# A last matrix product in fp32 by seven half-size products in place of eight

## The chip, the cores and the metric

One core of a Trainium2 chip runs the whole program as one launch. The metric is the device time of that launch in microseconds (us). Shorter is better. The kernel before was timed three times, with a median of 1404.88 us (1404.58 to 1405.83).

## What is computed

The program is a two-layer encoder for 1024 tokens of 1024 features, in float32. Layer A (an mLSTM beside a pooling mixer) comes first, then layer C, an attention layer with 8 heads of 128 features. The change concerns only the end of layer C, its output projection and the residual:

```
def mla_layer(x, ...):                       # x: (1, 1024, 1024)
    ...
    o = block_causal_attention(q, k, v).reshape(B, S, C_WIDTH) * jax.nn.silu(z)
    return x + o @ w_out                     # w_out: (1024, 1024)
```

So the last step is out = x1 + O W, with O (tokens by features) of 1024 by 1024 and W of 1024 by 1024. x1 is the output of layer A.

## The kernel before

**Products.** TensorE multiplies float32 numbers that are rounded to a shorter format. To keep float32 precision the kernel writes each operand as a sum hi + lo of two rounded numbers (`split`, L153 to L161: hi is a rounding copy on POOL or on ACT, lo = src - hi is a subtraction on DVE), and computes three matmuls hi·hi, hi·lo and lo·hi per block (`mm3`, L172 to L178), all into one PSUM bank. One matmul takes 128 features by 128 tokens against 128 features by 512 columns.

**Layer C.** The eight heads of attention run one after the other. While head h computes, `ahead(h)` feeds in pieces of what head h+1 needs, and during the last head (h = 7) the generator `out_ahead` (L1228) loads and splits the first operands of the output projection. Every head's gated output z is stored to a scratch array oz_d in HBM (L1198, SP's DMA queue); this is O transposed, features by tokens. It comes back from there as the left operand. Per head, a row of key norms goes over POOL (`rk`, L213), SP's queue out to HBM (`rk_d`, L1071) and back as `rkb` (L1072), and the head's scores are scaled by it (L1158).

**Output projection before** (L1276 to L1312). Eight feature tiles k, eight token tiles j and two column halves ch make 8 x 16 blocks of three matmuls, 384 in all. Operands are rows of 128 features by 1024: eight of O (`os` split into `oh`, `ol`) and eight of W (`w_st` split into `w_hi`, `w_lo`; the first three, `woh` and `wol`, by `out_ahead`). All loads there go out on ACT's queue. The first 192 matmuls run k by k over eight PSUM banks (so that operands can arrive while PE works), the other 192 bank by bank. Each bank is evicted by one DVE addition with a row of x1 (`x1r`, L1311) and stored by SP (L1312).

**Order.** The source's order isn't the engines' order. A scheduler, which runs at build time, reorders the instructions of each engine (`TC_KW = dict(schedule_with_timeline_sim=True)`). On the chip each engine runs its queue strictly in that order and waits on semaphores where an operand is not ready or a buffer is not free.

Of the kernel before, what the change touches and what calls it, by code (L numbers as in the profile page):

```python
# [19 lines left out]
P = 128  # L20
# [28 lines left out]
OUT_AHEAD = 3  # L49
# [7 lines left out]
def _parts(value, bits, n):  # L57
    """value as a sum of n numbers of at most `bits` significant bits each."""
# [30 lines left out]
def _hybrid(ctx, tc, nc, ins, consts, out, dbg):  # L89
# [20 lines left out]
    # ---------------------------------------------------------------- constants  # L110
# [52 lines left out]
    def split_scaled(hi, lo, src, scale):  # L163
        """src * scale = hi + lo; src in PSUM, scale a number or a column."""
# [7 lines left out]
    def mm3(acc, terms, start=True, stop=True):  # L172
        """acc (+)= sum of lhs.T @ rhs over terms ((lhs_hi, lhs_lo), (rhs_hi, rhs_lo))."""
# [8 lines left out]
    def wload(shape, src, hi_eng="pool", own=None, into=None):  # L182
        """A block of weights, or of other operands, loaded and split."""
# [25 lines left out]
    def rstd_of(dst, ssq, n):  # L209
        """dst = (ssq / n + eps) ** -0.5 for small tiles."""  # L210
# [7 lines left out]
    # ================================================================ layer A  # L218
# [29 lines left out]
    def om_tile(h, sig, ws, j):  # L248
        """sigmoid(om) of a head for 128 tokens; with the last head's columns the gates too."""
# [12 lines left out]
    # ---- x normalised, transposed and split, and the first head's output gate on its heels  # L262
# [57 lines left out]
    def feat_pieces(c0, use, w=None):  # L320
        """128 columns of the projection, features on partitions: use(half, psum) per half."""
# [27 lines left out]
    def conv(h, c, xm):  # L349
        """SiLU of the causal convolution of a chunk."""  # L350
# [23 lines left out]
    def windows(g, x0s, half):  # L374
        """Trailing means less the value itself, split, for half of the tokens."""
# [44 lines left out]
    def gate_math():  # L420
# [4 lines left out]
        # Scratch in the room of tiles that come later.  # L425
# [13 lines left out]
        # log_sigmoid(f) = min(f, 0) - log1p(exp(-|f|))  # L439
# [10 lines left out]
        # Sums of log f within a tile of 128 tokens, and over whole tiles.  # L450
# [19 lines left out]
        # The running maximum within a tile, one (tile, head) per partition; then over tiles.  # L470
# [876 lines left out]
```

## Time and profile before

| what | value |
|---|---|
| median of three runs | 1404.88 us |
| span of the profiled execution (first to last instruction) | 1403.8 us, 1.1 us under that median |
| PE busy | 1374.9 us, 98% of the span |
| DVE / ACT / POOL busy | 755.2 / 475.0 / 412.0 us |
| granted TensorE clock, mean | 0.997 |
| first matmul of the output projection (f_ps) starts | 1309.39 us |
| last eviction of it (x1r) starts | 1400.20 us |

The output projection is `f_ps` in the trace, its evictions are `x1r<-f_ps,x1r` on DVE. The engines are PE (matmul), PEld (weight load), DVE, ACT, POOL and SP. In a timeline a row gives start, duration, engine, line, operation, output and inputs, and in brackets how long the engine sat idle before and what released it. A row "x3" stands for three instructions in a row, and its duration is the stretch that they take together. Of the profiled execution the page gives the span alone; what lies around it is set at the 1.1 us above.

### The profile page before, as it was taken

To read this page: it belongs to the slowest core of one execution; us is meant where nothing else is said; L and a number is where in the kernel's file an instruction comes from. 1 tells how busy PE (TensorE), PEld (TensorE's weight loads), DVE (VectorE), ACT (ScalarE), POOL (GpSimd) and SP (SyncE) were. 2 spreads that over 40 slices of the span, in tenths; PEclk is the share of its full clock that TensorE was granted. 3 is DMA by queue.
4 is the path that set the end of the run, shared out by engine and by line. 5 is a ranking of instruction groups with operands and counts; after the bars stand their busy time and mean duration, and the time that the engine had idled before them with its cause. 6 is when DMAs were issued, how large, how long until landed. Compare 5 with 4: busy or idle time off the path is not lost.

```text
span 1403.8 us, 20224 instructions
## 1 busy us (share of the span) xinstructions
PE 1374.9 (98%) x7740; PEld 1205.8 (86%) x7740; DVE 755.2 (54%) x1616; ACT 475.0 (34%) x1146; POOL 412.0 (29%) x546
## 2 busy tenths in 40 slices
PE   7999999999999999999999999999989999999998
PEld 6888789888998889888888889988889999988887
DVE  6686544663365544653655333640167777878631
ACT  5433223331432223320001112421376667675200
POOL 3155213441144212321533111420153324151310
PEclk9999999999999999999999999999999999999999
DMA  5122311133022311127834232231311211122541
GB/s 198 39 81 64 101 53 48 55 94 97 16 80 60 102 53 53 51 74 253 301 106 150 90 88 78 73 103 53 104 34 54 67 54 54 57 80 69 217 157 53
DMA packets 101406, 126.88 MB, mean 90 GB/s; under 512 B 6231, under 2 KB 72510, under 8 KB 101310
## 3 DMA queue, kind: packets, MB, share of 16 engines
q1 hardware_dynamic: 98574, 115.63, 25.9%
q10 hardware_dynamic: 2736, 9.96, 2.0%
q8 instruction: 61, 1.00, 0.3%
q14 instruction: 35, 0.29, 0.1%
HBM read 100.34 MB, written 25.24 MB: 89 GB/s over the span
## 4 chain that ended last, share of the span: by engine, by line
PE 88%; DVE 4%; POOL 2%; issue 2%; DMA 2%; ACT 2%; SPq 0%; DVEq 0%; ACTq 0%; POOLq 0%
PE fp_ps L178 8%; PE fp_ps L177 8%; PE fp_ps L176 8%; PE s_ps L1155 5%; PE o_ps L176 4%; PE o_ps L178 4%; PE o_ps L177 4%; PE z_ps L178 2%; PE z_ps L177 2%; PE z_ps L176 2%; PE f_ps L178 2%; PE f_ps L176 2%; PE f_ps L177 2%; PE om_ps L177 2%; PE om_ps L178 2%; PE om_ps L176 2%
## 5 line engine op out<-in xcount | busy, mean ns | idle before, releaser
L156 POOL TENSOR_SCALAR w_hi<-w_st 128x1024 fp32r<-128x1024 f32 (+4 forms) x131 | 134.2, 1025 | 555.8 <-PE fp_ps L177 136.7
L161 DVE TENSOR_TENSOR w_lo<-w_st,w_hi 128x1024 fp32r<-128x1024 f32 (+4 forms) x131 | 156.2, 1194 | 221.7 <-POOL w_hi L156 221.7
L178 PE MATMUL fp_ps<-xnh,w_lo 128*128 128x512 f32 x512 | 202.6, 398 | 0.8 <-DVE w_lo L161 0.7
L177 PE MATMUL fp_ps<-xnl,w_hi 128*128 128x512 f32 x512 | 202.6, 396 | 0.0
L176 PE MATMUL fp_ps<-xnh,w_hi 128*128 128x512 f32 x512 | 202.1, 395 | 0.1
L178 PEld LDWEIGHTS fp_ps<-xnh,w_lo 128*128 128x128 f32 x512 | 96.1, 188 | 23.3 <-DVE w_lo L161 2.0
L176 PEld LDWEIGHTS fp_ps<-xnh,w_hi 128*128 128x128 f32 x512 | 97.2, 190 | 21.9 <-DVE zp L407 0.3
L177 PEld LDWEIGHTS fp_ps<-xnl,w_hi 128*128 128x128 f32 x512 | 96.2, 188 | 21.9
L178 PE MATMUL o_ps<-w_hi,yl 128*128 128x512 f32 x256 | 100.6, 393 | 0.0
L177 PE MATMUL o_ps<-w_lo,yh 128*128 128x512 f32 x256 | 100.4, 392 | 0.0
L176 PE MATMUL o_ps<-w_hi,yh 128*128 128x512 f32 x256 | 99.3, 395 | 0.0
L176 PE MATMUL om_ps<-w_hi,xnh 128*128 128x256 f32 (+1 forms) x256 | 73.1, 287 | 1.2 <-POOL w_hi L156 1.1
L177 PE MATMUL om_ps<-w_lo,xnh 128*128 128x256 f32 (+1 forms) x256 | 73.1, 287 | 0.1
L178 PE MATMUL om_ps<-w_hi,xnl 128*128 128x256 f32 (+1 forms) x256 | 73.0, 286 | 0.0
L1162 ACT ACTIVATE sp<-sp,mx,rq 128x128 f32<-128x128 f32 (+3 forms) x64 | 55.5, 867 | 22.3 <-DVE mx L1161 21.8
L178 PEld LDWEIGHTS o_ps<-w_hi,yl 128*128 128x128 f32 x256 | 48.1, 188 | 11.2
L177 PEld LDWEIGHTS o_ps<-w_lo,yh 128*128 128x128 f32 x256 | 48.1, 188 | 10.8
L176 PEld LDWEIGHTS o_ps<-w_hi,yh 128*128 128x128 f32 x256 | 48.1, 188 | 10.7
L170 DVE TENSOR_TENSOR ptl<-pT_ps,pth 128x512 fp32r<-128x512 f32 (+2 forms) x96 | 51.2, 548 | 6.1 <-ACT pth L169 6.0
L176 PEld LDWEIGHTS om_ps<-w_hi,xnh 128*128 128x128 f32 x256 | 49.1, 192 | 2.0 <-POOL w_hi L156 1.5
L176 PE MATMUL z_ps<-x1h,w_hi 128*128 128x512 f32 x128 | 50.7, 396 | 0.0
L178 PE MATMUL z_ps<-x1h,w_lo 128*128 128x512 f32 x128 | 50.7, 397 | 0.0
(364 smaller groups left out, 3594.3 us busy)
## 6 DMA issues: line engine op xcount, KB each, us to landing
w_st<-in_a_w_in_dram SPq DMA_DIRECT2D x38, 512.0 KB
w_st<-in_a_w_out_dram SPq DMA_DIRECT2D x32, 512.0 KB
w_st<-y_d SPq DMA_DIRECT2D x16, 512.0 KB
rb<-rr_d SPq DMA_DIRECT2D x8, 640.0 KB
x_t<-in_x_dram SPq DMA_DIRECT2D x8, 512.0 KB
y_d<-zp SPq DMA_DIRECT2D x16, 256.0 KB
y_d<-xc SPq DMA_DIRECT2D x16, 256.0 KB
x1t<-in_x_dram SPq DMA_DIRECT2D x8, 512.0 KB
```

Of the source, the lines that this page charges most:

```text
L156: i = G.tensor_scalar(hi, src, 1.0, 1.0, ALU.mult, ALU.mult)
L161: return i, V.tensor_tensor(lo, src, hi.bitcast(F32), ALU.subtract)
L170: V.tensor_tensor(lo, src, hi.bitcast(F32), ALU.subtract)
L176: T.matmul(acc, lh, rh, start=start and i == 0, stop=False)
L177: T.matmul(acc, lh, rl, start=False, stop=False)
L178: T.matmul(acc, ll, rh, start=False, stop=stop and i == n - 1)
L1155: T.matmul(ps[:, 0:w], l[:, js], r_[:, cs], start=i == 0, stop=i == 4)
L1162: A.activation(sp[:, 0:n], sp[:, 0:n], AF.Exp, bias=mx[:, 2:3], scale=rq[:, jt:jt + 1], accum_out=mx[:, 3:4])
```

## The change

The two operands are cut into halves, 512 by 512 each. Write the four blocks of O as early/late tokens (e, l) by low/high features, and those of W as low/high features (up, down) by left/right columns. Seven products of such blocks (the Winograd form of Strassen's scheme) replace the eight: each has 4 feature tiles t by 4 token tiles j by 3 matmuls = 48, and 7 x 48 = 336 matmuls stand in place of 384. They run in the order 1, 6, 7, 4, 5, 3, 2. Products 1 and 6 run feature tile by feature tile over four banks, the others bank by bank.

What the products need besides is sums of blocks, all of 128 by 512 per feature tile. On the W side: T1 = right - left of the upper half, T2 = right of the lower half - T1, a further left of the lower half - T2 for product 4 (in place, called T2' below), and right - right for product 7 (in place); these are POOL `tensor_tensor` instructions, 16 in all. On the O side: S1 = le + he, S2 = S1 - ll, ll - le (in place, le' below) and hl - S2, 16 DVE instructions. Each sum, or plain block, is then split as before, hi on ACT for the O side (`fxh`) and on POOL for the W side (`fwh`), lo on DVE for both (`fxl`, `fwl`). On the output side some products serve several outputs: product 1 is copied by ACT to `f_u` and added by POOL; product 6 and 7 are added to `f_u` on DVE, and `f_u` to the rows of x1 by POOL (8) and DVE (4); product 5 is added twice. The residual rows x1r are all loaded ahead.

`out_ahead` now loads all eight rows of W unsplit (`wo_raw`) and half of four rows of O, and computes T1 and the splits of product 1, where it loaded and split three rows of W and two of O.

```diff
-            for k in range(OUT_AHEAD):
-                st = wq_own[0].tile([P, wq_own[1]], F32, name="wo_st", tag="w_st", bufs=1)
-                SY.dma_start(st[:, 0:D], w_out[k * P:(k + 1) * P, :])
-                split(wh[:, k, :], wl[:, k, :], st[:, 0:D])
...
+            for k, (r, i) in zip(order_, place):
+                SY.dma_start(r[:, i, :], w_out[k * P:(k + 1) * P, :])
+                wr[k] = r[:, i, :]
+                if k < KD // 2:
+                    SY.dma_start(al[k // 2][:, k % 2, :].bitcast(F32), oz_d[k * P:(k + 1) * P, HALF:S])
                 yield
...
+            for t in range(KD // 2):
+                up = wr[t]
+                T1.append(t1[:, t, :])
+                G.tensor_tensor(T1[t], up[:, HALF:D], up[:, 0:HALF], ALU.subtract)
+                b = (bh[t // 2][:, t % 2, :], bl[:, t, :] if t < 2 else bl2[t - 2][:])
+                split(b[0], b[1], up[:, 0:HALF])
+                a = (ah[t // 2][:, t % 2, :], al[t // 2][:, t % 2, :])
+                split(a[0], a[1], a[1].bitcast(F32))
+                first.append((a, b))
+                yield
...
+            G.tensor_tensor(T2[t], wr[t + KH][:, right], T1[t], ALU.subtract)
+
+        for t in range(KH):
+            for k in (t, t + KH):
+                A.dma_start(xe[k][:], oz_d[k * P:(k + 1) * P, early])
+        for k in range(KD):
+            SY.dma_start(xl_[k][:], oz_d[k * P:(k + 1) * P, later])
+            if k == KH - 1:
+                for j in range(4, NT):
+                    SY.dma_start(xr[j][:], x1_d[j * P:(j + 1) * P, :])
...
+            elif p == 6:
+                S1.append(fsum(fo, "fs1", le, he, ALU.add, V))
+                S2.append(fsum(fo, "fs2", S1[t], ll, ALU.subtract, V))
+                src = S2[t]
             else:
...
+                V.tensor_tensor(le, ll, le, ALU.subtract)
+                src = le
+            return operand(fo, "fx", src, "act")
...
+            elif p == 4:
+                G.tensor_tensor(T2[t], down[:, left], T2[t], ALU.subtract)
+                src = T2[t]
...
+        def done1(j, ps):
+            A.copy(us[j][:], ps[:])
+            add(4 + j, left, us[j][:], G)
+
+        def done6(j, ps):
+            V.tensor_tensor(us[j][:], ps[:], us[j][:], ALU.add)
+            add(4 + j, right, us[j][:], G)
+
+        def done7(j, ps):
+            V.tensor_tensor(us[j][:], ps[:], us[j][:], ALU.add)
+            add(j, left, us[j][:], G)
+            add(j, right, us[j][:], V)
+
+        def done4(j, ps):
+            add(j, left, ps[:], V)
+            store(j, left)
...
+        product(1, done1, True)
+        product(6, done6, True)
+        product(7, done7)
+        product(4, done4)
+        product(5, done5)
+        product(3, done3)
+        product(2, done2)
```

How the scheduler then orders two of the engines is seen in the rows of their queues. The first place is DVE from the last multiplication of attention on (`z<-po,z`). Before, the rows there are these (`ol` and `w_lo` are the lo parts of an O row and a W row, each 128x1024):

```order
L1197 TENSOR_TENSOR z_12944<-po,z_12944 128x256
L161 TENSOR_TENSOR ol_12986<-os,oh_12985 128x1024
L161 TENSOR_TENSOR w_lo<-w_st,w_hi 128x1024
L161 TENSOR_TENSOR ol<-os,oh 128x1024
L161 TENSOR_TENSOR w_lo<-w_st,w_hi 128x1024 x3
L161 TENSOR_TENSOR ol<-os,oh 128x1024
L161 TENSOR_TENSOR w_lo<-w_st,w_hi 128x1024
L161 TENSOR_TENSOR ol<-os,oh 128x1024 x3
L1311 TENSOR_TENSOR x1r<-f_ps,x1r 128x512 x16
```

Now they begin like this (`fwl<-fsum,fwh` is the lo part of T2 for product 6, `fwl<-wo_raw` of product 7; `fsum<-oz_e` is S1, `fsum<-fsum,oz_l` is S2, `oz_e<-oz_l,oz_e` is le', `fxl<-fsum,fxh` is the lo part of S2 for product 6):

```order
L1196 TENSOR_TENSOR z_12965<-po,z_12965 128x256
L160 TENSOR_TENSOR fwl<-fsum,fwh 128x512 x4
L160 TENSOR_TENSOR fwl<-wo_raw,fwh 128x512 x2
L1306 TENSOR_TENSOR fsum<-oz_e 128x512
L1306 TENSOR_TENSOR fsum<-fsum,oz_l 128x512
L1349 TENSOR_TENSOR oz_e<-oz_l,oz_e 128x512
L1306 TENSOR_TENSOR fsum<-oz_e 128x512
L1306 TENSOR_TENSOR fsum<-fsum,oz_l 128x512
L1349 TENSOR_TENSOR oz_e<-oz_l,oz_e 128x512
L160 TENSOR_TENSOR fxl<-fsum,fxh 128x512 x2
```

Eleven lo parts and 16 evictions became 96 instructions of 128x512, of which 68 read both inputs from SBUF and 28 read one from PSUM. The lo part that completes product 6's first operand is now the thirteenth instruction behind the z multiplication.

The second place is POOL from the last head on. Before (`rk` is the key norms of the last head; `o_st` and `os` are rows of O):

```order
L156 TENSOR_SCALAR oh_12578<-o_st 128x1024
L213 TENSOR_TENSOR rk<-rk,mhalf 128x8
L156 TENSOR_SCALAR oh_12578<-o_st 128x1024
L156 TENSOR_SCALAR oh_12985<-os 128x1024
L156 TENSOR_SCALAR w_hi<-w_st 128x1024
L156 TENSOR_SCALAR oh<-os 128x1024
L156 TENSOR_SCALAR w_hi<-w_st 128x1024 x3
```

Now (`wo_raw<-wo_raw` is right - right for product 7; the first `fsum<-wo_raw,fsum` row is T2, the second T2'; `x1r<-f_u,x1r` adds product 1 to the rows of x1):

```order
L1368 TENSOR_TENSOR wo_raw<-wo_raw 128x512
L212 TENSOR_TENSOR rk<-rk,mhalf 128x8
L1368 TENSOR_TENSOR wo_raw<-wo_raw 128x512 x2
L155 TENSOR_SCALAR fxh<-fxl 128x512 x2
L1319 TENSOR_TENSOR fsum<-wo_raw,fsum 128x512 x4
L155 TENSOR_SCALAR fwh<-fsum 128x512 x4
L155 TENSOR_SCALAR fwh<-wo_raw 128x512 x2
L1361 TENSOR_TENSOR fsum<-wo_raw,fsum 128x512 x4
L1388 TENSOR_TENSOR x1r<-f_u,x1r 128x512 x4
```

T1, two of product 7's sums and six of the eight hi parts of product 1 stand ahead of `rk` in POOL's queue now, and eight `tensor_tensor` instructions follow T2's and product 7's first hi parts. On PE, 23 matmuls of f_ps stand ahead of the end of attention's last group both before and after; 361 follow it before, 313 now. On ACT's queue the eight loads of `oz_e` stand directly ahead of the four copies of product 1 to `f_u`, and those ahead of the first `fxh`. In head 6, eight loads of 128x1024 or 128x512 (six of W, two of O) stand on SP's queue ahead of the load of `rkb`, where two of 128x1024 stood. Behind the last head four loads of `oz_l`, four of `x1r`, four of `oz_l` and four of `x1r` follow the last store to oz_d on SP's queue.

More of the change, by code (lines that the diff above doesn't have):

```diff
@@ new lines, in out_ahead @@
+            place = [(r, i) for r in raw for i in range(r.shape[1])]
+            order_ = [v for t in range(KD // 2) for v in (t, t + KD // 2)]
+            t1 = lc.tile([P, KD // 2, HALF], F32, name="fsum", tag="ckl", bufs=1)
+            al = [wq_own[0].tile([P, 2, HALF], F32R, name="fxl", tag=tag, bufs=1) for tag in ("w_st", "w_hi")]
+            bh = [wq_own[0].tile([P, 2, HALF], F32R, name="fwh", tag="w_lo", bufs=1),
+                  ap_.tile([P, 2, HALF], F32R, name="fwh", tag="qnh", bufs=3)]
@@ L1247, in _hybrid @@
         w_out = ins["c_w_out"][0]
-        wo, os_ = [], []
+        wr, T1, first = [], [], []
         run(kv1, 3)
@@ L1274, in _hybrid @@
             after.pop()()
+    KH = KD // 2
+    later, early = slice(HALF, S), slice(0, HALF)
+    left, right = slice(0, HALF), slice(HALF, D)
     with ExitStack() as octx:
-        wpool["now"] = (octx.enter_context(pool("weights_o")), D, 4, KD - OUT_AHEAD)
-        wpool["queue"] = A
-        op = octx.enter_context(pool("cout"))
-        for k in range(2, KD):
-            if k >= OUT_AHEAD:
-                wo.append(wload([P, D], w_out[k * P:(k + 1) * P, :]))
-            st = op.tile([P, S], F32, name="os", bufs=2)
-            A.dma_start(st[:], oz_d[k * P:(k + 1) * P, :])
-            if k == 2:
-                oh = lc.tile([P, S], F32R, name="oh2", tag="kroh", bufs=1)
-                ol = lc.tile([P, S], F32R, name="ol2", tag="krol", bufs=1)
-            else:
-                oh = op.tile([P, S], F32R, name="oh", bufs=KD - 3)
-                ol = op.tile([P, S], F32R, name="ol", bufs=KD - 3)
-            split(oh[:], ol[:], st[:])
-            os_.append((oh, ol))
@@ L1294, in _hybrid @@
[L1294 to L1312 removed]
+        fr = octx.enter_context(pool("cout_w", side="right"))
@@ new lines, in _hybrid @@
+        fo = octx.enter_context(pool("cout"))
+        T2, xe, xl_, S1, S2 = [], [None] * KD, [None] * KD, [], []
+        xr = [fo.tile([P, D], F32, name="x1r", tag=f"x1r{j}", bufs=1) for j in range(NT)]
+        us = [fo.tile([P, HALF], F32, name="f_u", tag=f"f_u{j}", bufs=1) for j in range(4)]
+        for k in range(KD):
+            xe[k] = fo.tile([P, HALF], F32, name="oz_e", tag=f"oze{k}", bufs=1)
+        for k in range(KD):
+            xl_[k] = fo.tile([P, HALF], F32, name="oz_l", tag=f"ozl{k}", bufs=1)
@@ new lines, in fsum, with operand @@
+        def fsum(p, tag, a, b, op, eng):
+            t = p.tile([P, HALF], F32, name="fsum", tag=tag, bufs=4)
+            eng.tensor_tensor(t[:], a, b, op)
+            return t[:]
+        def operand(p, what, src, hi_eng):
+            hi = p.tile([P, HALF], F32R, name=f"{what}h", tag=f"{what}h", bufs=7 if p is fo else 6)
+            lo = p.tile([P, HALF], F32R, name=f"{what}l", tag=f"{what}l", bufs=6)
+            split(hi[:], lo[:], src, hi_eng)
+            return hi[:], lo[:]
+        for t, (tag, i) in enumerate((("kroh", 0), ("kroh", 1), ("krol", 0), ("krol", 1))):
+            if i == 0:
+                t2 = lc.tile([P, 2, HALF], F32, name="fsum", tag=tag, bufs=1)
+            T2.append(t2[:, i, :])
+            G.tensor_tensor(T2[t], wr[t + KH][:, right], T1[t], ALU.subtract)
@@ new lines, in product @@
+        def product(p, done, t_major=False):
+            ops = first if p == 1 else [(a_op(p, t), b_op(p, t)) for t in range(KH)]
+            pss = {}
+            steps = [(t, j) for t in range(KH) for j in range(4)] if t_major else [(t, j) for j in range(4) for t in range(KH)]
+            for t, j in steps:
+                (ah, al), (bh, bl) = ops[t]
+                js = slice(j * P, (j + 1) * P)
+                if t == 0:
+                    bank, tag = (ptr, "tr") if t_major and j == 3 else (pmm, "mm")
+                    pss[j] = bank.tile([P, 512], F32, name="f_ps", tag=tag)
+                mm3(pss[j][:], [((ah[:, js], al[:, js]), (bh, bl))], start=t == 0, stop=t == KH - 1)
+                if t == KH - 1:
+                    done(j, pss[j])
@@ new lines, in add, with store @@
+        def add(row, cs, src, eng):
+            r = xr[row][:, cs]
+            eng.tensor_tensor(r, src, r, ALU.add)
+        def store(row, cs):
+            SY.dma_start(out_d[row * P:(row + 1) * P, cs], xr[row][:, cs])
+        def done1(j, ps):
[8 more added lines that the diff above has]
+            add(j, right, us[j][:], V)
```

75 lines of the change are left out of this document (45 added, 30 removed).

## The prediction

> **What bounds the kernel now.** I read the page's busy shares first, then windows over the end, then the timelines of the engines that feed PE there. Part 1 of the page:
>
> ```profile
> span 1403.8 us, 20224 instructions
> PE 1374.9 (98%) x7740; PEld 1205.8 (86%) x7740; DVE 755.2 (54%) x1616; ACT 475.0 (34%) x1146; POOL 412.0 (29%) x546
> ```
>
> PE is the bound on average. Windows over the end of the program show whether that holds where the change is:
>
> ```profile
> core 0: us, PE busy (x) PEld busy (x) DVE busy (x) ACT busy (x) POOL busy (x), PEclk, DMA share, GB/s
> 1311.00:1318.00 7.00, 7.00 (x44) 6.25 (x43) 0.44 (x2) 0.00 (x0) 3.64 (x4) 1.00 1.01 369
> 1320.00:1340.00 20.00, 20.00 (x90) 16.54 (x89) 12.65 (x9) 0.00 (x0) 8.05 (x6) 1.00 0.65 237
> 1340.00:1360.00 20.00, 20.00 (x90) 16.51 (x89) 6.68 (x9) 0.00 (x0) 1.05 (x1) 1.00 0.36 119
> 1360.00:1380.00 20.00, 20.00 (x89) 16.38 (x88) 2.76 (x4) 0.00 (x0) 0.00 (x0) 1.00 0.36 137
> 1380.00:1404.00 24.00, 20.16 (x88) 16.16 (x87) 2.77 (x4) 0.00 (x0) 0.00 (x0) 0.99 0.14 51
> ```
>
> In the output projection PE never waits (20.00 of 20.00), and the other engines have less and less to do. So each matmul taken away there is worth its whole time, as long as PE stays fed. What one costs is read from the evictions of the second half, one per 24 matmuls (DVE's timeline, first and last row):
>
> ```profile
> 1361.66 0.69 DVE L1311 TENSOR_TENSOR x1r<-f_ps,x1r 128x512 f32<-128x512 f32 x1 [4.82 <-DMA x1r<-x_d]
> ...
> 1400.20 0.69 DVE L1311 TENSOR_TENSOR x1r<-f_ps,x1r 128x512 f32<-128x512 f32 x1 [4.81 <-PE f_ps L178]
> ```
>
> Seven intervals take 38.54 us: 5.51 us per 24 matmuls, 0.2295 us each.
>
> **Part 1: 48 matmuls fewer.** 384 - 336 = 48, of the same 128x512 form: 48 x 0.2295 = **-11.0 us**. What lies behind the last matmul (one DVE addition, one store) stays as it is.
>
> **Part 2: product 6 starts hungry.** PE passes attention's last group at 1317.5, just ahead of DVE's z row below. 25 of product 1's matmuls are left then (48 - 23), so PE wants product 6 at 1317.5 + 25 x 0.2295 = 1323.2. What must be ready is S2 and T2, both split. DVE and POOL at this place before:
>
> ```profile
> 1317.71 0.42 DVE L1197 TENSOR_TENSOR z<-po,z 128x256 f32<-128x256 f32 x1 [6.56 <-PE po L178]
> 1318.05 1.58 DVE L161 TENSOR_TENSOR ol<-os,oh 128x1024 fp32r<-128x1024 f32 x1
> 1319.56 2.06 DVE L161 TENSOR_TENSOR w_lo<-w_st,w_hi 128x1024 fp32r<-128x1024 f32 x1
> 1321.54 2.06 DVE L161 TENSOR_TENSOR ol<-os,oh 128x1024 fp32r<-128x1024 f32 x1
> 1323.53 3.48 DVE L161 TENSOR_TENSOR w_lo<-w_st,w_hi 128x1024 fp32r<-128x1024 f32 x3
> ```
>
> ```profile
> 1317.51 1.05 POOL L156 TENSOR_SCALAR w_hi<-w_st 128x1024 fp32r<-128x1024 f32 x1
> 1318.79 3.74 POOL L156 TENSOR_SCALAR w_hi<-w_st 128x1024 fp32r<-128x1024 f32 x2 [0.23 <-DMA w_st<-in_c_w_out_dram]
> ```
>
> This is the row pair that decides my forecast. Alone, a lo part takes 1.16 us (3.48 for three) and a POOL split 1.05. While both engines work, a lo part takes 2.06 with a pitch of 1.98 (1319.56 to 1321.54), and a POOL split 1.87. Two of each take some 4 us either way: the engines take turns. A pair of 128x512 is half of that, 1.0 us. For POOL's `tensor_tensor` of 128x512 the nearest rows are the pooling of layer A (columns: min/median/max ns), and beside them a DVE operation with one input from PSUM:
>
> ```profile
> L384 POOL TENSOR_TENSOR pa<-pa x24: 1050/1060/1550, 77.4 to 446.5; 128x524 f32<-128x524 f32 x12, 128x520 f32<-128x520 f32 x8, 128x512 f32<-128x512 f32 x4
> L161 DVE TENSOR_TENSOR ml<-pa,mh x16: 677/692/1570, 116.1 to 604.1; 128x512 fp32r<-128x512 f32 x16
> L170 DVE TENSOR_TENSOR ptl<-pT_ps,pth 128x512 fp32r<-128x512 f32 x48 | 32.3, 682 | 4.5 <-ACT pth L169 4.5
> L1311 DVE TENSOR_TENSOR x1r<-f_ps,x1r 128x512 f32<-128x512 f32 x16 | 11.0, 691 | 47.1 <-PE f_ps L178 42.2 <-DMA x1r<-x_d 4.8
> ```
>
> So a `tensor_tensor` takes 1.06 alone and up to 1.55 beside DVE, a DVE operation with both inputs in SBUF 0.69 alone and up to 1.57: one of each takes 1.55 in turns. The PSUM readers keep 0.68 and 0.69 on average. [...]
>
> The timetable, in the order of the queues: DVE ends z at 1318.1. Five lo parts beside POOL's hi parts, 1.0 each: 1323.1. Then POOL has the four T2' and four additions of product 1 to x1 (eight of 1.06), and DVE's next eight operations run beside these at 1.55. The sixth lo part, S1 and S2 of the first feature tile: 1327.8. Then ACT's copy:
>
> ```profile
> 1299.78 0.56 ACT L169 CAST pth<-pT_ps 128x512 fp32r<-128x512 f32 x1
> ```
>
> 0.6 later, at 1328.4, the first hi part is there: PE has waited 1328.4 - 1323.2 = 5.2 us. It has eight matmuls then that need no lo part of S2 (two terms, four banks), 1.8 us, to 1330.2. The lo part `fxl` comes after le', S1, S2, le': five operations, 5 x 1.55, 1335.5. PE waits another 5.3 us. Together **+10.5 us**. The loads that feed this come in time or nearly, by these rows (the last stores to oz_d, the oz loads then, and one load of 512 KB from issue to use):
>
> ```profile
> 1304.89 13.58 SPq L1198 DMA_DIRECT2D oz_d<-z  x3
> 1271.27 0.38 SPq L1242 DMA_DIRECT2D o_st<-oz_d  x1
> 1275.31 1.41 POOL L156 TENSOR_SCALAR oh<-o_st 128x1024 fp32r<-128x1024 f32 x1 [1.57 <-DMA o_st<-oz_d]
> ```
>
> The last store is issued at about 1318.2, the first `oz_l` load behind it, at 1318.5, lands by 1318.5 + 4.0 = 1322.5 at the latest (it is half as large), ahead of its use at 1326. The x1r loads wait for product 1's end (their room) and land at about 1327.5, before POOL reaches the additions at 1329. ACT's queue holds eight loads of `oz_e`, of which the last waits for the last store to land (1318.2 + some 2) and then for a free slot; I put its end at 1323.5, the four copies of product 1 at 1325.8. Without turns between DVE and POOL this would be the bound: first hi part at 1326.4, a wait of 3.1 us, and no second one. So the ends for this term are 3.1 and 10.5; I take 10.5, since the pair of rows above lies exactly at this place.
>
> **Part 3: the clock.** The granted clock fell once within the program, at a gap of PE (a window, and PE's row behind the gap):
>
> ```profile
> 1038.00:1045.00 7.00, 6.08 (x28) 5.92 (x29) 4.96 (x20) 4.52 (x13) 1.65 (x1) 0.52 0.12 37
> 1038.75 0.45 PE L1181 MATMUL pT_ps<-ident,sp 128*128 128x128 f32 x1 [1.96 <-DVE sp L1164]
> ```
>
> A gap of 1.96 us was followed by some 7 us at half the clock. Gaps of 5 us are more likely to do so. The first gap's slow matmuls end inside the second wait. The second would cost half of 3.4 to 7 us, 1.7 to 3.5; none if the clock holds. I take **+2.5 us**. Product 6 (40 matmuls left, 9.2 us) then ends at 1335.5 + 9.2 + 2.5 = 1347.2, product 7 (11.0) at 1358.2.
>
> **Part 4: product 4's third block.** Product 7 finds its operands ready. In product 4, 24 matmuls on two feature tiles come first; 1358.2 + 5.6 = 1363.8 is when PE wants the third W block. From 1335.5 to its lo part DVE has 26 operations (eight of them PSUM evictions) and POOL eight hi parts and eight `tensor_tensor`: 26 x 0.65 + 8 x 0.55 (half of 1.05) + 8 x 1.06 = 29.8 us if all are in turns, to 1365.3. An eviction of product 7's last bank is queued just ahead of it, so it can't come before 1359 in any case. Wait: **+1.5 us**; 0 if turns cost less, 3.7 if the clock holds (PE then arrives 2.5 earlier, so parts 3 and 4 cover for each other). Products 5, 3, 2 need fewer operations on DVE (eight splits each and four to eight evictions in 11.0 us) and I cost their feeding at nothing; PE covers it.
>
> **Part 5: the last heads of attention.** The key norms of head 7 are late, since POOL has T1 and the early splits ahead of `rk`:
>
> ```profile
> 1272.09 1.65 POOL L213 TENSOR_TENSOR rk<-rk,mhalf 128x8 f32<-128x8 f32 x1 [2.87 <-DVE rk L211]
> 1278.30 0.29 SPq L1071 DMA_DIRECT2D rk_d<-rkr  x1
> 1280.80 0.33 SPq L1072 DMA_DIRECT2D rkb<-rk_d  x1
> ```
>
> One T1 waits for a W row that is loaded at about 1275; with it, two more 1.06 and a 0.55 stand ahead, so `rk` ends near 1279 instead of 1273.7. How much of a late `rkb` shows is seen in the idle time that DVE spent before its use, over all heads:
>
> ```profile
> its engine sat idle before it (us, times) until:
> ...
>   DMA rkb<-rk_d: 4.2, 5
> ```
>
> DVE waits for it already in five of eight heads, so some lateness will show; but 4.6 us lie between the end of `rk` and its store, which doesn't wait for `rk` alone, and they absorb part of the 5 us: I take **+1.5 us** for this and for head 6's `rkb`, which queues behind eight loads in place of two. The bounds are -1 (three fewer lo parts on DVE in head 7) and +4 (nothing absorbed).
>
> **Sum.** -11.0 + 10.5 + 2.5 + 1.5 + 1.5 = +5.0 us: a span of 1408.8, and with the 1.1 us between span and median, **1409.9 us**.
>
> **Rivals.**
>
> (a) DVE and POOL hardly hinder each other, or the turns fall elsewhere. Then product 6 waits 3.1 us, the clock holds, part 4 is nothing: -11.0 + 3.1 + 1.5 = -6.4, **1398.5 us**, faster. It decides the case if the first `fxl` of product 6 ends before 1330. For it: the median of the `ml` row is 0.69, so most of these met no POOL operation that held them. Against it: the pair at 1319.56.
>
> (b) The same with the turns half as costly, a first wait of 5 us and a second of 2, no clock drop: -11.0 + 7 + 1.5 + 1.5 = -1.0, **1403.9 us**, no change. [...]
>
> (c) Head 7's scores come late by all of 5 us less what DVE saves there, and attention adds 4, the clock the full 3.5: -11.0 + 10.5 + 3.5 + 1.5 + 4 = +8.5, **1413.4 us**. For it: the 4.2 us of waits for `rkb`. Against: the 4.6 us ahead of its store.
>
> **Chances.** 0.2% of the time before, 2.8 us, is about what a measurement of this kernel can tell from no change: 1402.1 to 1407.7 counts as the same. My forecast has 0.45, (a) 0.23, (b) 0.22, (c) 0.10. The forecast's own range, from parts 3 and 4, is 1406.5 to 1413; a small part of it (0.03) lies under 1407.7. Faster 0.23, same 0.25, slower 0.52. The range from (a) to a little above (c) is 1398.4 to 1414.5.
>
> **What would show it.** Right: PE gaps of about 5 us, twice, early in product 6, ended by ACT's `fxh` and DVE's `fxl`; DVE's S1, S2, le' at 1.5 us each between POOL's T2' and x1r rows; a stretch at clock 0.5 behind the second gap; a short gap in product 4; `rk` of head 7 some 5 us later with little of it on the scores. Wrong: S1 and S2 at 0.69 beside busy POOL, one PE gap of about 3 us ended by ACT or a DMA, and DVE idle before product 4.

## The result, and the profile after

The changed kernel takes 1418.82 us in the median of four runs (1418.48 to 1419.26), the kernel before 1405.18 beside it: a ratio of 1.0095, 95% interval 1.0081 to 1.0110. It is slower by 13.6 us, where about 5 were forecast, and the time lies above the range. Page of the profiled execution after:

```profile
span 1416.8 us, 20356 instructions
PE 1371.4 (97%) x7692; PEld 1199.3 (85%) x7692; DVE 809.5 (57%) x1688; ACT 491.9 (35%) x1174; POOL 458.2 (32%) x590
```

PE is busy for 3.5 us less and the span is 13.0 us longer: PE waits. Windows over the end (from the end of attention on):

```profile
core 0: us, PE busy (x) PEld busy (x) DVE busy (x) ACT busy (x) POOL busy (x), PEclk, DMA share, GB/s
1320.00:1330.00 10.00, 6.88 (x34) 5.36 (x33) 5.77 (x6) 1.31 (x3) 8.33 (x9) 0.99 0.71 220
1330.00:1340.00 10.00, 3.75 (x8) 2.49 (x8) 9.93 (x8) 1.98 (x4) 8.48 (x6) 0.50 0.99 385
1340.00:1350.00 10.00, 8.89 (x27) 7.04 (x28) 9.88 (x16) 3.85 (x7) 1.72 (x2) 0.66 0.42 169
1350.00:1360.00 10.00, 10.00 (x45) 8.03 (x44) 10.00 (x14) 1.25 (x2) 6.29 (x6) 1.00 0.01 2
1360.00:1370.00 10.00, 10.00 (x45) 8.02 (x44) 10.00 (x11) 3.11 (x5) 10.00 (x8) 1.00 0.00 1
1370.00:1380.00 10.00, 8.21 (x29) 6.22 (x28) 10.00 (x14) 1.87 (x3) 5.48 (x6) 0.83 0.01 5
```

Before, PE had 20.00 of 20 here. Now DVE has hardly any idle time from 1330 to 1380 (9.93, 9.88, then 10.00 of 10), and PE falls short where DVE is late. PE's three long waits are these rows of its timeline, in products 6, 6 and 4:

```profile
1334.59 0.77 PE L175 MATMUL f_ps<-fwh,fxh 128*128 128x512 f32 x1 [7.71 <-ACT fxh L157]
...
1341.11 2.08 PE L177 MATMUL f_ps<-fwh,fxl 128*128 128x512 f32 x4 [2.77 <-DVE fxl L160]
...
1372.81 0.50 PE L176 MATMUL f_ps<-fwl,fxh 128*128 128x512 f32 x1 [1.79 <-DVE fwl L160]
```

They stand where the prediction put them. Behind the first and the third the granted clock is half: 0.50 in the window of 1330, and 0.83 in that of 1370, where a window from 1374.2 to 1377.4 alone shows 0.50. A matmul then takes 0.43 us from start to start instead of 0.2334. The DVE rows that make the first wait, from attention's last z on:

```profile
1321.00 0.42 DVE L1196 TENSOR_TENSOR z<-po,z 128x256 f32<-128x256 f32 x1 [6.62 <-PE po L177]
1321.69 2.10 DVE L160 TENSOR_TENSOR fwl<-fsum,fwh 128x512 fp32r<-128x512 f32 x2 [0.27 <-POOL fwh L155]
1326.76 2.31 DVE L160 TENSOR_TENSOR fwl<-fsum,fwh 128x512 fp32r<-128x512 f32 x2 [2.96 <-POOL fsum L1361]
1328.99 3.42 DVE L160 TENSOR_TENSOR fwl<-wo_raw,fwh 128x512 fp32r<-128x512 f32 x2
1332.33 0.68 DVE L1306 TENSOR_TENSOR fsum<-oz_e 128x512 f32<-128x512 f32 x1
1333.05 0.69 DVE L1306 TENSOR_TENSOR fsum<-fsum,oz_l 128x512 f32<-128x512 f32 x1
1333.65 1.76 DVE L1349 TENSOR_TENSOR oz_e<-oz_l,oz_e 128x512 f32<-128x512 f32 x1
1335.34 1.76 DVE L1306 TENSOR_TENSOR fsum<-oz_e 128x512 f32<-128x512 f32 x1
1337.13 1.65 DVE L1306 TENSOR_TENSOR fsum<-fsum,oz_l 128x512 f32<-128x512 f32 x1
1338.70 1.75 DVE L1349 TENSOR_TENSOR oz_e<-oz_l,oz_e 128x512 f32<-128x512 f32 x1
1340.37 1.28 DVE L160 TENSOR_TENSOR fxl<-fsum,fxh 128x512 fp32r<-128x512 f32 x2
```

And POOL beside them:

```profile
1325.41 2.50 POOL L1361 TENSOR_TENSOR fsum<-wo_raw,fsum 128x512 f32<-128x512 f32 x2
1328.55 3.32 POOL L1361 TENSOR_TENSOR fsum<-wo_raw,fsum 128x512 f32<-128x512 f32 x2 [0.63 <-DVE fwl L160]
1333.28 6.62 POOL L1388 TENSOR_TENSOR x1r<-f_u,x1r 128x512 f32<-128x512 f32 x4 [1.42 <-DMA x1r<-x_d]
```

Two things are seen. The first: where POOL has a sum, a DVE operation takes 1.65 to 1.76, and they follow each other every 1.70 us (two in 3.42 us); S1 and S2 in the 1.4 us in which POOL waited for x1r take 0.68 and 0.69. The operations with an input from PSUM aren't held up so here: of the four evictions in the next row, which follow each other every 0.60 us, the last three run beside POOL's additions:

```profile
1354.99 2.48 DVE L1398 TENSOR_TENSOR f_u<-f_ps,f_u 128x512 f32<-128x512 f32 x4
1355.76 9.43 POOL L1388 TENSOR_TENSOR x1r<-f_u,x1r 128x512 f32<-128x512 f32 x6 [0.21 <-DVE f_u L1398]
```

The second thing is that DVE stood idle for 2.96 us from 1323.8. It isn't `fwh` that it waited for: POOL's four hi parts of T2 end at 1324.3. The wait ends at 1326.76, just behind the start of product 1's last matmul at 1326.49, and in e_nopool, below, the profile names PE's f_ps matmuls as its end. The room of the third lo part is still held by product 1's operands. I had not seen that wait.

Attention's last z moved from 1317.71 to 1321.00.

### The profile page after: what moved, and what is told of

The parts are those of the page before. It is cut to its first block, busy times and chain, and to the rows that moved or that the text cites. A ratio compares the mean times of both kernels' runs of the same rounds, so it can differ in the third digit from the quotient of the medians.

```text
span 1416.8 us, 20356 instructions
## 1 busy us (share of the span) xinstructions
PE 1371.4 (97%) x7692; PEld 1199.3 (85%) x7692; DVE 809.5 (57%) x1688; ACT 491.9 (35%) x1174; POOL 458.2 (32%) x590
## 4 chain that ended last, share of the span: by engine, by line
PE 87%; DVE 6%; ACT 2%; issue 2%; DMA 2%; POOL 1%; SPq 0%; DVEq 0%; ACTq 0%; POOLq 0%
PE fp_ps L177 8%; PE fp_ps L176 8%; PE fp_ps L175 8%; PE s_ps L1154 6%; PE o_ps L175 4%; PE o_ps L177 4%; PE o_ps L176 4%; PE z_ps L176 2%; PE z_ps L177 2%; PE z_ps L175 2%; PE om_ps L176 2%; PE om_ps L177 2%; PE om_ps L175 2%; PE pT_ps L1180 2%; PE f_ps L177 2%
## 5 line engine op out<-in xcount | busy, mean ns | idle before, releaser
L155 POOL TENSOR_SCALAR w_hi<-w_st 128x1024 fp32r<-128x1024 f32 (+4 forms) x126 | 128.1, 1017 | 555.6 <-PE fp_ps L176 138.2
L160 DVE TENSOR_TENSOR w_lo<-w_st,w_hi 128x1024 fp32r<-128x1024 f32 (+4 forms) x126 | 149.9, 1191 | 223.5 <-POOL w_hi L155 223.5
L1180 PE MATMUL pT_ps<-ident,sp 128*128 128x128 f32 x288 | 44.1, 278 | 9.2 <-DVE sp L1163 3.6
L175 PE MATMUL f_ps<-fwh,fxh 128*128 128x512 f32 x112 | 45.5, 417 | 7.7 <-ACT fxh L157 7.7
L168 ACT CAST pth<-pT_ps 128x512 fp32r<-128x512 f32 (+2 forms) x96 | 43.4, 477 | 25.7 <-PE pT_ps L1180 24.0
```

Of the source, the lines that this page charges most:

```text
L155: i = G.tensor_scalar(hi, src, 1.0, 1.0, ALU.mult, ALU.mult)
L160: return i, V.tensor_tensor(lo, src, hi.bitcast(F32), ALU.subtract)
L168: A.copy(hi, src)
L175: T.matmul(acc, lh, rh, start=start and i == 0, stop=False)
L1180: T.transpose(ps[:, i * P:(i + 1) * P], sp[:, (4 * blk + i) * P:(4 * blk + i + 1) * P], ident[:])
```

## The experiments

All but two start from the changed kernel. The median is given beside the run of the kernel before on the same chip. "Tail" is the time from the start of the last matmul of attention (po) to the end of the last f_ps matmul in the profiled execution, which leaves the attention out. 313 matmuls at 0.2334 and 0.4 for the last one's end are 73.5 us; what is above is wait or slow clock.

| run | median, us (before) | last z | tail | PE's waits behind product 1 |
|---|---|---|---|---|
| kernel before | 1405.18 | 1317.7 | 82.8 | none |
| changed | 1418.82 (1405.18) | 1321.0 | 92.2 | 7.9, 3.2, 2.0 |
| e_nopool | 1411.99 (1404.89) | 1321.5 | 85.5 | 4.7, 3.4 |
| e_nofwl | 1411.90 (1405.20) | 1321.5 | 85.1 | 4.7, 1.3, 1.5, 1.2 |
| e_act | 1412.65 (1405.23) | 1321.0 | 84.9 | 8.4, 0.8 |
| e_dveadd | 1413.17 (1405.23) | 1321.4 | 86.5 | 6.4, 2.2, 1.2 |
| e_both | 1410.75 (1405.23) | 1320.9 | 84.1 | 8.1, 0.7 |
| e_both_order | 1408.50 (1405.23) | 1321.7 | 84.1 | 2.9, 3.5 |
| e_order | 1417.79 (1404.89) | 1322.0 | 90.1 | 4.5, 1.9, 2.1, 1.0, 2.0, 0.4 |
| e_fill2 | 1420.20 (1405.20) | 1323.3 | 92.3 | 3.6, 0.7, 4.6 (and 72 filling matmuls) |
| e_fill | 1420.37 (1404.89) | 1319.2 | 93.5 | 4.8, 2.7 (and 36 filling matmuls) |
| e_noT | 1417.88 (1404.89) | 1319.2 | 93.4 | 7.9, 2.1, 4.2 |
| e_nolo1 | 1419.92 (1405.20) | 1322.5 | 92.9 | 6.1, 3.2, 3.9 |
| e_min | 1411.14 (1405.26) | 1315.7 | 93.1 | 6.1, 3.2, 3.7 |
| e_gap (from the kernel before) | 1415.58 (1405.20) | 1318.1 | 91.1 | 6.5, the hole |
| e_pitch (from the kernel before) | 1405.61 (1405.26) | 1318.0 | 82.8 | none |

The waits are start-to-start distances of successive f_ps matmuls above 0.6 us, less 0.233 (the stretch of the filling matmuls left out). The last z differs by up to 4.1 us between profiled runs with the same attention (1319.2 in e_fill, 1323.3 in e_fill2; 2.4 of it are there already at a z near 1247: 1245.9 and 1248.3), and spans differ from medians by up to 4 us. So mechanisms are read from the tail and its rows, and totals from the medians.

**Do DVE and POOL hold each other up?** Taking eight POOL sums away:

```diff
-                G.tensor_tensor(T2[t], down[:, left], T2[t], ALU.subtract)
                 src = T2[t]
...
             A.copy(us[j][:], ps[:])
-            add(4 + j, left, us[j][:], G)
```

> The changed kernel without eight POOL instructions that stand beside product 6's feeding: the four T2' (product 4 then takes T2 in its place) and the four additions of product 1 to x1. The order on DVE stays. Theory of turns (DVE and POOL hold each other up): the six DVE operations from product 1's end to S2 fall from 1.7 to 0.6-0.7 us where they met these, PE's first wait in product 6 from 7.9 to about 5, the second from 3.0 to under 1, and the span from 1416.8 to 1408-1411. Rival, queue and buffers alone (DVE has the weights' lo parts ahead of S1 and S2, and these wait for product 1's end): the operations keep their times, first wait 7 or more, span 1415 or more.

DVE's timeline, at the same operations as above:

```profile
1327.26 1.29 DVE L160 TENSOR_TENSOR fwl<-fsum,fwh 128x512 fp32r<-128x512 f32 x2 [2.95 <-PE f_ps L176]
1328.47 1.29 DVE L160 TENSOR_TENSOR fwl<-wo_raw,fwh 128x512 fp32r<-128x512 f32 x2
1329.67 0.68 DVE L1306 TENSOR_TENSOR fsum<-oz_e 128x512 f32<-128x512 f32 x1
1330.39 0.69 DVE L1306 TENSOR_TENSOR fsum<-fsum,oz_l 128x512 f32<-128x512 f32 x1
1331.00 0.68 DVE L1349 TENSOR_TENSOR oz_e<-oz_l,oz_e 128x512 f32<-128x512 f32 x1
```

Every operation is at 0.68 or 0.69, pairs at 1.29, the tail is 6.7 us shorter, the first wait 4.7 instead of 7.9, the second gone. Theory of turns, as expected (span 1410.5), though product 4's wait grew from 2.0 to 3.4. The rest of the first wait stays: the idle 2.95 before product 1's end is here too, now put down to PE. The next run takes the operations behind that idle time away, and leaves POOL as it is (in products 6 and 7 no lo part of W is computed, the hi part stands in its place):

```diff
+            if p in (6, 7):
+                hi = fr.tile([P, HALF], F32R, name="fwh", tag="fwh", bufs=6)
+                G.tensor_scalar(hi[:], src, 1.0, 1.0, ALU.mult, ALU.mult)
+                return hi[:], hi[:]
             return operand(fr, "fw", src, "pool")
```

> The changed kernel without the lo parts of W in products 6 and 7 (eight DVE operations fewer; the hi part takes their place). Six of them stand in DVE's queue ahead of S1 and S2, four of these wait for product 1's end. Theory (the first wait of product 6 is DVE's queue, its wait for product 1's buffers, and turns with POOL): S2 is ready at 1326-1329 instead of 1333.7, the first wait falls from 7.9 to 0-3 us, span 1405-1409. Rival (the loads of oz_e and oz_l come late anyway): the first wait stays at 5 or more.

S2 is ready early, at 1327.3 (the end of DVE's first row here), but ACT turns it into `fxh` only at 1331.13:

```profile
1325.93 1.40 DVE L1306 TENSOR_TENSOR fsum<-fsum,oz_l 128x512 f32<-128x512 f32 x1 [3.23 <-DMA oz_l<-oz_d]
1327.25 1.74 DVE L1349 TENSOR_TENSOR oz_e<-oz_l,oz_e 128x512 f32<-128x512 f32 x1
```

```profile
1323.89 5.23 ACTq L1323 DMA_DIRECT2D oz_e<-oz_d  x5
1329.21 2.05 ACT L1398 COPY f_u<-f_ps 128x512 f32<-128x512 f32 x4 [15.17 <-DMA oz_e<-oz_d]
1331.13 0.65 ACT L157 CAST fxh<-fsum 128x512 fp32r<-128x512 f32 x1
```

ACT's queue is issuing its last five loads until 1329.1 (what holds them up isn't shown), then ACT does product 1's four copies. So the expectation of 0 to 3 us was wrong: behind DVE's queue lies ACT's, which ends the first wait at 4.7, where the prediction's rival (a) had put 3.1. In e_nopool the two come out together: ACT's copies end at 1331.0 and S2 at 1331.1. The tail is 7.1 us shorter nevertheless; eight DVE operations are gone.

**POOL's work elsewhere.** The hi parts on ACT and the oz_e loads on SP:

```diff
-                A.dma_start(xe[k][:], oz_d[k * P:(k + 1) * P, early])
+                SY.dma_start(xe[k][:], oz_d[k * P:(k + 1) * P, early])
...
-            return operand(fr, "fw", src, "pool")
+            return operand(fr, "fw", src, "act")
```

> The changed kernel with the 24 hi parts of W blocks of products 6 to 2 on ACT in place of POOL, and the oz_e loads on SP's queue in place of ACT's (they would hold ACT's hi parts up). POOL keeps its sixteen sums. Theory of turns: each POOL hi part costs DVE 0.45 us (a pitch of 1.05 in place of 0.61); 10 to 14 of them lie in the stretch from product 1's end to product 4, in which DVE is never idle, so product 4's third block comes 4-6 us earlier: span 1410-1413. Rival (ACT or the loads become the late ones): 1415 or more.

Tail 84.9, product 4's wait 0.8: as expected. (The edit moves the loads too, and the first wait is 8.4, so it isn't the hi parts alone.) The other way, POOL's sums on DVE (T2' in the same manner):

```diff
-            add(4 + j, left, us[j][:], G)
+            add(4 + j, left, us[j][:], V)
...
-            add(4 + j, right, us[j][:], G)
+            add(4 + j, right, us[j][:], V)
```

> The changed kernel with the sixteen POOL sums behind attention (four T2', twelve additions to x1) on DVE; the hi parts stay on POOL. DVE has 16 instructions more. Theory of turns: a sum costs DVE 0.61 when DVE does it itself and 1.06-1.1 when POOL does it, so DVE comes out ahead by about 16 x 0.45 = 7 us by product 4: span 1409-1412. Rival (DVE's count alone is the bound and POOL takes work off it): 16 x 0.61 = 10 us later, span 1420 or more.

DVE has 16 instructions more and the tail is 5.7 us shorter, as the theory of turns said and against the rival. This is the run that tells most: a sum that DVE does itself costs it less than one that POOL does beside it. Both edits together:

> Both of the edits before: POOL has nothing to do behind attention. Theory of turns: DVE's operations with two SBUF inputs all at 0.61-0.69; PE's first wait in product 6 about 5 us (the order of DVE's queue and product 1's buffers stay), no wait in product 4, half clock once: span 1403-1407. Rival: DVE with 112 instructions of 0.61-0.69 is still the bound in product 4, span 1409 or more.

```profile
1340.00:1350.00 10.00, 10.00 (x45) 8.03 (x44) 10.00 (x17) 3.86 (x8) 0.00 (x0) 1.00 0.59 231
1350.00:1360.00 10.00, 10.00 (x45) 8.03 (x44) 10.00 (x18) 2.98 (x7) 0.00 (x0) 1.00 0.00 1
1360.00:1370.00 10.00, 10.00 (x44) 8.03 (x43) 10.00 (x18) 5.20 (x10) 0.00 (x0) 1.00 0.00 1
```

In these windows POOL has nothing, DVE does 17 or 18 operations in 10 us (11 to 14 in the changed kernel from 1350 to 1380) and PE is never without work. The first wait came out at 8.1 instead of 5, so the span was 1408.6 and not 1403-1407: DVE's queue had got all four T2' and three further S1 ahead of S2, which ended at 1333.9. The median, 1410.75, is at the rival's edge, but its reason isn't seen: PE had no wait in product 4.

**Product 2 ahead of product 6.** In the changed kernel, and then with both edits:

```diff
         product(1, done1, True)
-        product(6, done6, True)
+        product(2, done2, True)
+        product(6, done6)
         product(7, done7)
...
-        product(2, done2)
```

> The changed kernel with product 2 moved from the last to the second place (its operands are plain blocks, no sum; the rows of O that it needs are loaded first). Theory (product 6 waits because 5.6 us of PE work cover too little of the sums and splits, and the slow clock follows from that wait): both waits and the half clock in product 6 go, span 1402-1406. Rival (DVE and POOL together have too much work from here to the end, in turns): the waits come back in products 6, 7 or 4, span 1409 or more.

> As before, and product 2 in the second place with its rows of O loaded first. Theory: product 2 covers the sums of product 6, PE waits 2-4 us at product 2's start, and nothing behind: span 1399-1403, at or below the kernel before. Rival (DVE can't get product 2's splits and product 6's sums ready in time): 1405 or more.

Alone it moved the waits to other places (tail 90.1): the rival. With POOL free it is the fastest form found, 1408.50 us, a ratio of 1.0025 (1.0013 to 1.0038) to the kernel before, and so the rival too (1405 or more, where 1399-1403 was expected). It still waits at products 2 and 6, and attention ends late; no run here beats the kernel before.

**The clock.** First by itself, in the kernel before, with a hole on PE between its two groups:

```diff
+            if j0 == 4:
+                g = op.tile([P, HALF], F32, name="hold", bufs=1)
+                V.tensor_tensor(g[:], xr[:, HALF:D], xr[:, HALF:D], ALU.max)
+                for _ in range(6):
+                    V.tensor_tensor(g[:], g[:], g[:], ALU.max)
+                for c in range(2):
+                    lo0 = os_[0][0][:, HALF + c * 256:HALF + (c + 1) * 256]
+                    V.scalar_tensor_tensor(lo0, g[:, 0:256], 0.0, lo0.bitcast(F32), ALU.mult, ALU.add)
```

> The kernel before with nothing but a hole on PE: between its two groups of four token tiles DVE has a chain of nine operations (a maximum of a tile with itself seven times, then k = 0's hi part of O written onto itself in two halves, the result unchanged), for which PE's next group waits, about 5 us. Theory of the clock: behind the hole the granted clock is 0.5 for 3 to 7 us, so the span grows by the hole and 1.7-3.5 us more, 1410-1412.5. Rival (a hole costs itself alone): 1408.5-1409.

```profile
1362.81 0.80 PE L176 MATMUL f_ps<-woh,oh 128*128 128x512 f32 x1 [6.33 <-DVE oh L1302]
1363.40 0.63 PE L177 MATMUL f_ps<-wol,oh 128*128 128x512 f32 x1
...
1366.39 0.47 PE L178 MATMUL f_ps<-woh,ol 128*128 128x512 f32 x1
1366.70 0.39 PE L176 MATMUL f_ps<-w_hi,oh 128*128 128x512 f32 x1
```

The hole was 6.5 us, and behind it matmuls start every 0.43 us until 1366.6, for 3.8 us: a cost of 1.8 us. The span is 8.7 us above the kernel before, 8.3 of them the hole and the slow clock, 0.4 from ahead of them. Theory of the clock, at the low end of its price; behind this hole PE had work. In the changed kernel PE kept waiting behind the first hole, and matmuls ran at half clock from 1334.6 to 1346.8 (a window from 1329.8 to 1346.8 shows 0.50); added up over the tail, slow matmuls took 5.8 us more than at 0.2334.

Then the clock's share in the changed kernel, with PE kept busy between products 1 and 6. The first filling matmuls used product 1's operands, whose room the x1r loads and with them SP's queue wait for (the x1r loads went out at 1333.6 instead of 1327.0, the next loads of O at 1337.2 instead of 1333.1), so that product 6 met late loads of O instead; it says nothing on the clock's price:

```diff
+        fill = ptr.tile([P, 512], F32, name="fill_ps", tag="tr")
+        (fa, _), (fb, _) = first[3]
+        for i in range(36):
+            T.matmul(fill[:], fa[:, 0:P], fb, start=i == 0, stop=i == 35)
```

> The changed kernel with 36 extra matmuls (8.4 us at full clock, into a PSUM bank that nobody reads) on PE between products 1 and 6, so that PE works while it would wait. Theory of the clock (the half clock after the wait costs time of its own): no granted clock of 0.5 at the start of product 6, product 6 ends at about 1351 instead of 1353 since DVE's lo parts then bound it, span 1412.5-1415. Rival (DVE alone sets the pace, the slow clock is hidden behind it): span 1416-1417.5.

The second time with a constant (`T.matmul(fill[:, 0:P], identr[:], identr[:], ...)`, 72 times):

> The changed kernel with 72 extra matmuls of a 128x128 constant (about 8.4 us, into a bank that nobody reads) on PE between products 1 and 6; unlike the filling tried before, they hold none of product 1's operands, so no buffer and no load waits for them. Theory of the clock: clock 1.0 at product 6's start; PE then runs into DVE's lo parts only, product 6 ends 2-3 us earlier. What of it reaches the end depends on product 4's wait, which DVE's work sets (it was 2.0 us): span 1413-1416. Rival (the slow clock hides entirely behind DVE): 1416.5-1417.5.

The clock stayed at 1.00 until product 4 (windows from 1320 to 1370), and the tail was 92.3 us, as without. What product 6 won, product 4 lost to the same DVE work:

```profile
1375.54 0.79 PE L176 MATMUL f_ps<-fwl,fxh 128*128 128x512 f32 x1 [4.44 <-DVE fwl L160]
```

So the half clock in product 6, about 4 us of it, costs nothing there: the rival's reason was right, though the span lies above its range too. (The span of 1419.2 is above the changed kernel's since attention ended 2.3 us later.)

**Attention.** Without T1 and right - right (products 5 to 7 take plain blocks):

```diff
-                G.tensor_tensor(T1[t], up[:, HALF:D], up[:, 0:HALF], ALU.subtract)
+                T1.append(up[:, HALF:D])
...
-                G.tensor_tensor(up[:, right], down[:, right], up[:, right], ALU.subtract)
```

> The changed kernel without T1 and without right - right for product 7 (eight POOL subtractions; products 5, 6, 7 take plain blocks of W in their place). These stand in the last head of attention, ahead of and behind rk. Theory (POOL's subtractions there delay rk and hold DVE up): the end of attention, 1321.0 in the changed kernel, falls back to 1317.5-1318.5, PE's wait of 2.2 us at 1281 is gone, span 1413-1414. Rival (the loads on SP's queue delay it): the end of attention stays at 1320 or later, span 1416 or more.

The last z came at 1319.2, but e_fill, which has the changed kernel's attention, has the same, and a wait of 2.2 us stayed. Measured from the z near 1247 to the last z, which leaves out what differs ahead of it, the kernel before takes 69.2 us, the changed kernel 73.6 and the runs with its attention 73.2 to 75.0. Here it is 72.3: about 1 us of the 4.4 belongs to these subtractions. Without the lo parts of product 1 (`b = (b[0], b[0])`):

> The changed kernel without the four lo parts of W in product 1 (the hi parts take their place), which DVE computes in the last heads of attention, three of them ahead of the key norms' copy rkr. Theory (these and POOL's sums beside them make PE wait 2.2 us at 1280, and half a clock follows): that wait and the slow stretch there go, attention ends 2-4 us earlier: span 1413-1415. Rival (rk's delay on POOL alone): the wait stays, 1416 or more.

The wait broke up (the longest from 1275 to 1300 is 0.95, and one of 1.51 comes at 1313), and the stretch from the z near 1247 is 74.0, no shorter: the theory in this form fell. With both, and with one feature tile split instead of four:

```diff
             for t in range(KD // 2):
...
+                if t == 0:
```

> The changed kernel with the least work left in the last heads of attention: no T1 and no right - right (as in the run without these), and only one feature tile of product 1 is split (product 1 uses it four times). The loads of W and O stay. Theory (the later end of attention comes from the operations that DVE and POOL got there): from the second last head's last z to the last z as in the kernel before within 1 us, attention ends by 1318. Rival (the eight loads ahead of rkb and what the scheduler made of head 7): the end stays at 1319 or later, with the wait of 2.2 us at 1280.

```profile
1315.69 0.43 DVE L1196 TENSOR_TENSOR z<-po,z 128x256 f32<-128x256 f32 x1 [6.60 <-PE po L177]
```

Attention ends at 1315.7, and from the z near 1247 it takes 68.9 us, as the kernel before (69.2), with the eight loads still ahead of `rkb`. So it is the work in the last heads, all of it together, and not the loads. One place where that work holds PE up is seen in the changed kernel at 1280, first DVE, then PE:

```profile
1277.98 1.28 DVE L160 TENSOR_TENSOR fwl<-wo_raw,fwh 128x512 fp32r<-128x512 f32 x2
1279.19 1.62 DVE L1163 TENSOR_SCALAR sp<-sp,mx 128x768 f32<-128x768 f32 x1
...
1281.31 0.26 DVE L1069 COPY rkr<-rk_ps 8x128 f32<-8x128 f32 x1
```

```profile
1281.62 0.84 PE L1180 MATMUL pT_ps<-ident,sp 128*128 128x128 f32 x4 [2.19 <-DVE rkr L1069]
```

Two lo parts and a softmax scaling of 1.62 (0.59 in the mean before, in its group of 128x768), which ran beside a POOL sum, hold up the copy that frees the bank for PE's next transposition. It is one place and not the whole cause: without this wait, in e_nolo1, attention ended no earlier. How the 4.4 us come about in all stays open.

**The price of one matmul.** In the kernel before, operands in tiles of 128x512 for five of eight k (`split(wh2[c][:], wl2[c][:], wst[:, c * HALF:(c + 1) * HALF])`, and so for O):

> The kernel before with the operands of k = 3 to 7 in tiles of 128x512 as in the changed kernel (two halves, split one by one) in place of 128x1024. Its matmuls are the same in number and order. In the changed kernel a matmul of the projection took 0.2334 us where it took 0.2270 to 0.2295 before. Theory (the width of the operands' tiles, or where the halves lie, makes it): the pitch goes to 0.233 for these five of eight, the last 300 matmuls take 1 us longer. Rival (something else in the changed kernel): pitch 0.227-0.2295, span within 0.5 us of the kernel before.

Median 1405.61 beside 1405.26, ratio 0.9999 (0.9987 to 1.0010), and the same 0.2267 to 0.2295 per matmul as before. The tiles' width isn't it. Why a matmul of the projection takes 0.2334 us in the changed kernel stays open. In the kernel before it isn't one number either: bank by bank the matmuls of k = 5 and 6 start every 0.227 us and those of k = 1 every 0.232.

## Why the prediction was wrong

The kinds of delay were right: turns between DVE and POOL, two waits early in product 6, half clock, a short wait in product 4, late attention. What failed is their sizing, above all the timetable of DVE's queue in parts 2 and 4, and part 5. Term by term, with what the tail shows on PE:

- **Part 1, -11.0 us.** Measured -9.3: 73.5 us for 313 matmuls at 0.2334 against 82.8 for 361 before. The step "of the same 128x512 form: 48 x 0.2295" took the form for the price.
- **Part 2, +10.5 us.** Measured 7.9 + 3.2 = 11.1. That the sum is near is luck, its parts are not right. DVE's third lo part waited 2.96 us for product 1's end, which my timetable let run through. The turns cost 1.70 per pair of sums and 1.05 per pair with a hi part, not 1.55 and 1.0. Against that, S1 and S2 of the first feature tile met no POOL sum that held them and took 0.68 and 0.69, not 1.55. Taken one after the other, by my estimate from rows in which one of the two engines works alone, a pair of sums would cost 0.61 (DVE in e_nopool, two from 1327.26 to 1328.47) + 1.06 (POOL's `pa` in the kernel before, the median) = 1.67, near the 1.70 measured, and a pair with a hi part 0.61 + 0.60 = 1.21 (POOL does two in 1.20 us with DVE idle, in the changed kernel at 1324.24), where 1.05 was measured.
- **Part 3, +2.5 us.** Measured 5.8 in the tail, in two stretches (about 4.2 from 1334.6 to 1346.8, and 1.6 behind product 4's wait), and one more in attention, where a window from 1280 to 1300 shows 0.91. The step "half of 3.4 to 7 us" was sized for a PE that has work again behind the hole; e_gap shows that price, 1.8. Of its two ends the kernel before shows the upper one alone (0.50 from 1038.3 to 1045.1, 6.8 us), the changed kernel the lower one too (3.4 us from 1374.1). Gaps of about 5 us and more did bring the half clock: behind PE's waits of 7.95 (e_both), 7.71 (changed kernel), 6.33 (e_gap), 4.56 (e_nopool) and 4.44 us (e_fill2) matmuls start every 0.42 to 0.43 us. On PE's account this is the largest miss, but e_fill2 shows that its larger part, in product 6, was hidden.
- **Part 4, +1.5 us.** Measured 2.0, and this is luck too. The prediction counts 26 DVE operations between the first `fxl` of product 6 and the lo part of product 4's third block; the trace has 39 (the windows show 41 from 1340 to 1370). They took 31.7 us, not much above the 29.8 forecast, since far from all met POOL: most of those from 1341.6 to 1355 took 0.68. That parts 3 and 4 cover for each other held: e_fill2 took the slow clock from product 6 and product 4's wait grew to 4.6.
- **Part 5, +1.5 us.** Measured 3.3 at the last z, and 4.4 from the z near 1247 on: the step that failed most in proportion. I priced the lateness of `rk` (it came 3.0 us later) and put the operations that POOL and DVE got in the last heads at nothing, or at a gain; e_min, without most of them, takes no longer there than the kernel before.

-9.3 + 11.1 + 5.8 + 2.0 + 3.3 = +12.9, where the span grew by 13.0.

This sum counts slow matmuls that hid behind DVE. Along DVE's way the 8.0 us between the forecast span (1408.8) and the measured one (1416.8) fall so. Attention's last z came 1.8 us later than forecast. From there to PE's first matmul with a `fxl` it took 20.1 us and not 17.8, from there to product 4's third block 31.7 and not 29.8, and from there to the last matmul's end 40.1 and not 38.4 (0.2334 per matmul, and the half clock behind product 4's wait). The last 0.3 lie behind it.

What the terms hide, and the experiments show, is that the tail is set in the main by one thing: DVE's queue, lengthened by its turns with POOL, from product 1's end to product 4's third block. At its start product 1's room and ACT's queue count too (the 4.7 of e_nofwl). Removing a wait on that way moves it (e_fill2, e_order, e_noT); removing turns or operations shortens it (e_nopool, e_dveadd, e_act, e_nofwl). Rivals (a), no mutual hindrance, and (b), turns half as costly, fell with the rows at 1.70. Rival (c), at 1413.4, came nearest, for its late attention and full clock cost.

## What to carry to other kernels

Fewer products pay only what the sums around them leave. Here 48 matmuls less bring 9.3 us at the price that a matmul has in the changed kernel, and the sums, splits and additions turn an end of the program in which DVE had time to spare into one in which it has none. Before moving sums to POOL to spare DVE, look how long DVE's operations take beside such a sum: here each POOL sum made a DVE operation with two inputs in SBUF 1.09 us longer (1.70 instead of 0.61), evictions from PSUM kept their 0.60, and doing the sum on DVE itself cost 0.61.
When a timetable is made by hand, ask of every queued instruction what still holds its output's room, and where two engines are seen to take turns, as DVE and POOL here (1.70 us for a pair of sums), add up the work of the pair before adding up waits.

## What was not expected of the hardware

- The same 128x512 fp32r matmul starts every 0.2267 to 0.2295 us, in the mean of 24, in the kernel before and every 0.2333 in the changed one, at a clock of 1.00 in both (windows of 24 from 1357.3 and from 1348.9), whether DVE is busy or not (5.60 of 5.60 us from 1348.9, 1.42 of 5.60 from 1402.9). The width of the operands' tiles is not the cause (e_pitch); nothing else was tried.
- After a PE hole with work behind it the half clock lasted another 3.8 us (e_gap, 1362.8 to 1366.6); with PE waiting on and off it lasted another 12 us (changed kernel, 1334.6 to 1346.8). In the changed kernel a wait of 1.79 us in product 4 and one of 2.19 us in attention were each followed by 3.4 us of half clock (0.50 from 1374.1 and from 1282.0), while in e_fill2 a wait of 3.6 us was followed by none (1.00 in the windows from 1330 to 1370). Nor did waits of one length act alike: one of 1.96 us was followed by 6.8 us at 0.50 in the kernel before (at 1038.75) and by none in the changed one (at 1040.22, 1.00 from 1040 to 1047), one of 1.78 us by none in the kernel before (at 147.72, 1.00 from 145 to 152) and by 3.4 us at 0.50 in the changed one (at 147.88). So in these runs the length of one wait doesn't decide it.
- A one-input DVE operation from SBUF (the scaling of 128x768, 0.59 us in the mean before) took 1.62 beside a POOL sum (changed kernel, at 1279.19), and one of 128x512 took 1.51 (at 1268.19; 0.52 in the mean before), so here the turns are not confined to operations with two SBUF inputs.
